# A two-block network on one core: the second block's tokens kept in residue-major order, and the low halves of the undilated keys kept twice

## The chip, the cores and the metric

The kernel runs on one core of a Trainium2 chip. The metric is the device time of one execution in microseconds (us). Three runs of the kernel before gave 2754.89, 2755.57 and 2758.86 us; their median, 2755.57 us, is the time that the change is measured against.

## The reference

A first block of two layers (a gated recurrent mixer, a convolution and a feed-forward part) turns 512 tokens of width 1024 into `x`. It is the same code before and after the change, up to its last norm. A second block follows, of two layers in float32. Their core is:

```python
def second_block(x, p, a_w_in, ...):
    cos, sin = rope_tables(x.shape[1])
    for i in range(2):
        h = mixer_a(x, ...) if i == 0 else mixer_b(x, ...)
        x = layer_norm(DEEPNORM_ALPHA * x + h, ln_g[i], ln_b[i])
        gate = sigmoid(x @ ple_w_gate[i])
        x = x + gate * (p[i] @ ple_w_proj[i])

def mixer_a(x, w_in, w_out, cos, sin):
    h = x @ w_in
    for gi, (window, dil) in enumerate(A_GROUPS):      # dil = 1, 4, 16
        q, k, v = ...                                  # 16 heads of 64, rope on q and k
        # tokens regrouped by their residue modulo dil, then a band of window // dil keys
        o, lse = banded_attention(strided(q), strided(k), strided(v), window // dil)
    o = the three groups' o, weighted by softmax(lse)
    return (o * silu(z)) @ w_out
```

`mixer_b` is a banded attention over neighbouring tokens (16 query heads, few key heads, a sink logit per head). So the undilated group of mixer A and mixer B look at blocks of 128 neighbouring tokens, while the groups with a stride look at tokens that are equal modulo 4.

## The kernel before

**Numbers.** Every float32 operand of a large product is split into a high and a low half of a narrower type (`split`: ScalarE copies the high half, VectorE subtracts it). A product of 128 rows of the contraction is three matmuls: high by high, high by low, low by high. A weight block comes by `wblock`: two loads of 512 KB into a ring of three `raw` tiles, each split into half of `hi` and `lo` when it has landed.

**Activations.** The input of mixer A is `HA = (Hh, Hl)`, feature-major: 8 tiles of 128 features by 512 tokens, high and low. The first block's last norm writes it in four chunks of 128 tokens (`chunkf`, `finish_T`): eight transposes of a chunk, and two splits into columns `128c` to `128c + 128`. The columns stand in the order of the tokens. `pend` holds these transposes back until a piece of mixer A asks for them (`pend.upto`).

**Mixer A** works through 12 steps, (Q, g): quads Q = 0 to 3 of four heads, and in each the groups g = 0 (undilated), 1 and 2 (dilated by 4 and 16; for both, keys are taken within a residue modulo 4, and a mask does the rest). A step (Q, g) has eight pieces of products, `a_pieces`: q and k, feature-major, two pieces each of 24 matmuls with 512 columns (weights stationary, tokens moving), and four pieces `v`, token-major, one for each block of 128 tokens, of 24 matmuls with 256 columns. In these the tokens are stationary:

```python
tk = slice(128 * b, 128 * b + 128) if g == 0 else slice(b, 512, 4)
tmj(lambda kc: (HA[0][:, kc, tk], HA[1][:, kc, tk]), wb[2], 0, 256, ps)
```

In g = 0 a block is 128 neighbouring columns, in g = 1 and 2 every fourth column. Step (0,0) does v first, then q and k; the others q and k first. Steps (1,0), (2,0), (3,0) do k before q.

Between a step's pieces `weave` puts the seven stages of the step before: scores with mask, maximum and exponentials of a head (`scores`: matmuls on PE, masked maximum on VectorE, exponentials on ScalarE), transposes of the exponentials, and the product with the values, whose result ScalarE evicts.

**Rotation.** When both halves of q or k are there, `rope` forms four products with cosine and sine on VectorE and two sums on POOL, and SP copies each in pieces of 32 partitions into the tile of heads. For g > 0 POOL's sum also reorders the tokens, from `4m+s` to `128s+m`. In the undilated steps of quads 1 to 3 `rope_split` does it with a split: q goes into two tiles `w`, where a head's high half stands beside its low half on 128 partitions; k goes into `kh`, with a head's high half kept twice, and `kl`, with its low half on 64 partitions. A score is then two matmuls: 128 rows (`kh`), and 64 rows (`kl`):

```python
return [(d[0][c][:, r, :], d[1][0][:, 2 * c + r, :]), (d[0][c][rows, r, :], d[1][1][rows, c, :])]
```

**What sets the order.** All DMAs, weights and these small copies alike, are issued by SP one after another (`ld`). A scheduler lays each engine's instructions in an order of its own when the program is built, so the order on ScalarE is not that of the code. The undilated results go to `o3`, those of g = 1 and 2 to tiles `w`; the results of a quad are weighted by `merge_stats` and the merges, which run beside the next quad. Where one group's layout differs from another's, the eviction or the merge reorders the tokens.

Then come the output product of mixer A, a layer norm, a gate, mixer B on the same scheme (undilated throughout, all its scores with 128 rows), and the same end, which writes the result.

Of the kernel before, what the change touches and what calls it, by code (L numbers as in the profile page):

```python
# [31 lines left out]
class Lane:  # L32
    """Background work: generators advanced a few steps at a time between foreground pieces."""
# [19 lines left out]
class Pending:  # L53
    """Deferred ends of a chain, run in order a few foreground pieces after their start."""
# [16 lines left out]
def emit(ctx, tc, a, out):  # L71
# [81 lines left out]
    # ---------------------------------------------------------------- helpers  # L153
# [42 lines left out]
    def fm_pair(wb, H, segs):  # L196
        """Both column chunks of a block, token range by token range as they become ready."""
# [17 lines left out]
    def wide(src, nk, lhs, chs, bank, use, pre=None, early=None, first=None):  # L215
        """Token-major product over 2*nk row blocks into 1024 columns, 512 columns and half of the rows at a time."""
# [24 lines left out]
    # ---------------------------------------------------------------- modulation  # L241
# [45 lines left out]
    def mod_start(pool, pool2, fill):  # L287
        """sh1 and sc1 of the first layer, streamed together."""
# [44 lines left out]
    def finish_T(pool, src, H, t0, A=None, B=None):  # L333
        """src: token-major chunk -> A*src+B, feature-major, split."""
        for i in range(2):
# [3 lines left out]
            if A is None:  # L339
                lasts["A"], lasts["V"] = split(H[0][:, 4 * i:4 * i + 4, t0:t0 + 128],  # L340
                                               H[1][:, 4 * i:4 * i + 4, t0:t0 + 128],
                                               pt.rearrange("p (m t) -> p m t", m=4))
                continue
# [15 lines left out]
    def rms(ss):  # L359
        """Reciprocal root mean square of each row."""  # L360
# [8 lines left out]
    def scaled(pool, xt, rs):  # L369
        """The rows times their factors, in two halves."""  # L370
# [46 lines left out]
    # ---------------------------------------------------------------- first block  # L417
# [3 lines left out]
    def projections(l, MIX, H, hook):  # L421
# [23 lines left out]
        # v and gates, chunk by chunk  # L445
# [18 lines left out]
        # convolution  # L464
# [29 lines left out]
        # gating unit  # L494
# [30 lines left out]
        def og_piece(h):  # L525
            """Output gate of one head."""
# [301 lines left out]
    def layer(l, H1, hside, oside, x_in, nn, mix_mods, ffn_mods):  # L828
# [83 lines left out]
        # output projection, second norm  # L912
# [46 lines left out]
        # feed forward  # L959
# [59 lines left out]
    # ---- start  # L1019
# [90 lines left out]
    def chunkf(h, c, xt, ss):  # L1110
# [6 lines left out]
        pend.add(c, lambda: finish_T(None, blocks(xt), h[1], 128 * c))  # L1117
# [4 lines left out]
    # ---------------------------------------------------------------- second block  # L1122
# [4 lines left out]
    def rope(RP, p1, p2, cs, perm, dst):  # L1127
        """p1, p2: [4 heads x 32, 512] halves; dst: [2 heads x 64, 2, 512]."""
# [14 lines left out]
    def rope_split(RP, p1, p2, cs, hi_to, lo_to):  # L1143
        """As rope, split; hi_to, lo_to: places (head, tile [128, slots, 512], first partition, slot) of the heads."""
# [14 lines left out]
    class Pair:  # L1159
        """Attention of two heads over 4 query blocks, in stages."""  # L1160
# [75 lines left out]
    def post_attention(i, Y, w_out, xin, sideh, first=None):  # L1236
# [8 lines left out]
        for c in range(4):  # L1245
            xt[c] = T(w6, [128, D], "w")
            ld(xt[c], xin[c])
# [556 lines left out]
```

## Time and profile before

| | |
|---|---|
| median of three runs | 2755.57 us (2754.89 to 2758.86) |
| span of the profiled execution | 2747.6 us |
| PE (TensorE matmuls) busy in it | 2669.2 us, 97% |
| VectorE, ScalarE, POOL busy | 1335.4, 965.2, 553.9 us (49%, 35%, 20%) |
| instructions in the span | 39361 |

The profile shows one execution. Its own time cannot be told from its span by what the trace holds; the median of the runs stands 8.0 us above the span, for what lies before the first and behind the last recorded instruction. PE is busy nearly all the time, so what the other engines do shows only where PE waits for it. `L138` is the one line that issues matmuls, `L121`, `L124` and `L159` are those that issue ScalarE's activations, tensor operations of VectorE and POOL, and DMAs, so groups are told apart by the names of their tiles: `mm` are accumulators of products (of `hi`, `lo` weights by `Hh`, `Hl`), `tr` those of scores and transposes, `md` those of the values, `sb` scores, `et` transposed exponentials.

### The profile page before, as it was taken

To read this page: it belongs to the slowest core of one execution; us is meant where nothing else is said; L and a number is where in the kernel's file an instruction comes from. 1 tells how busy PE (TensorE), PEld (TensorE's weight loads), DVE (VectorE), ACT (ScalarE), POOL (GpSimd) and SP (SyncE) were. 2 spreads that over 40 slices of the span, in tenths; PEclk is the share of its full clock that TensorE was granted. 3 is DMA by queue.
4 is the path that set the end of the run, shared out by engine and by line. 5 is a ranking of instruction groups with operands and counts; after the bars stand their busy time and mean duration, and the time that the engine had idled before them with its cause. 6 is when DMAs were issued, how large, how long until landed. Compare 5 with 4: busy or idle time off the path is not lost.

```text
span 2747.6 us, 39361 instructions
## 1 busy us (share of the span) xinstructions
PE 2669.2 (97%) x15288; PEld 2249.5 (82%) x15288; DVE 1335.4 (49%) x2802; ACT 965.2 (35%) x2017; POOL 553.9 (20%) x574
## 2 busy tenths in 40 slices
PE   7999999999999989999999999999999999999998
PEld 5888798778888878878788887887988888778786
DVE  5665744223332256565434334434535444675666
ACT  3323544111211153344322224324233333533753
POOL 1165531011011040043100002211302112021102
PEclk9999999999999999999999999999999999999999
DMA  8311644541222132145422223323323233425442
GB/s 295 116 62 53 203 147 156 194 140 62 63 67 70 51 109 69 62 141 197 146 92 92 93 92 130 97 77 108 108 77 108 83 110 100 142 95 155 121 166 77
DMA packets 125754, 311.04 MB, mean 113 GB/s; under 512 B 17120, under 2 KB 45376, under 8 KB 125568
## 3 DMA queue, kind: packets, MB, share of 16 engines
q1 hardware_dynamic: 125568, 308.53, 35.2%
q8 instruction: 121, 1.98, 0.3%
q14 instruction: 65, 0.53, 0.1%
HBM read 272.02 MB, written 13.89 MB: 104 GB/s over the span
## 4 chain that ended last, share of the span: by engine, by line
PE 82%; DVE 6%; DMA 4%; POOL 3%; ACT 3%; issue 2%; SPq 0%; POOLq 0%; DVEq 0%; ACTq 0%
PE mm L138 69%; PE tr L138 5%; PE md L138 5%; PE tr L1214 1%; DMA wm<-in_w_mod_dram 1%; DVE w L124 1%; DMA t<-mwd 1%; DVE lo L124 1%; POOL w L124 1%; ACT hi L121 1%; POOL rs L124 1%; ACT t L121 1%; POOL t L124 1%; DVE t L124 0%; DVE xs L131 0%
## 5 line engine op out<-in xcount | busy, mean ns | idle before, releaser
L138 PE MATMUL mm<-Hh,hi 128*128 128x512 f32 (+1 forms) x2168 | 790.9, 365 | 0.5 <-ACT Hh L121 0.4
L138 PE MATMUL mm<-Hl,hi 128*128 128x512 f32 (+1 forms) x2168 | 763.5, 363 | 0.0
L138 PE MATMUL mm<-Hh,lo 128*128 128x512 f32 (+1 forms) x2168 | 708.0, 364 | 0.0
L121 ACT ACTIVATE hi<-raw 128x1024 fp32r<-128x1024 f32 (+2 forms) x334 | 337.5, 1041 | 803.9 <-PE mm L138 445.3
L124 DVE TENSOR_TENSOR lo<-raw,hi 128x1024 fp32r<-128x1024 f32 (+2 forms) x334 | 429.1, 1305 | 317.7 <-ACT hi L121 317.5
L138 PEld LDWEIGHTS mm<-Hh,hi 128*128 128x128 f32 x2168 | 408.6, 189 | 96.9 <-issue 4.3
L138 PEld LDWEIGHTS mm<-Hl,hi 128*128 128x128 f32 x2168 | 408.4, 188 | 67.4 <-issue 0.6
L138 PEld LDWEIGHTS mm<-Hh,lo 128*128 128x128 f32 x2168 | 373.4, 189 | 47.4 <-issue 3.0
L124 POOL TENSOR_TENSOR w<-w,ot 128x256 f32<-128x256 f32 x160 | 128.5, 822 | 913.6 <-DVE ot L124 907.9
L124 DVE TENSOR_TENSOR sg<-mm,sg 128x512 f32<-128x512 f32 (+1 forms) x132 | 75.6, 599 | 408.9 <-PE mm L138 235.2
L138 PE MATMUL mm<-hi,Hh 128*128 128x256 f32 (+2 forms) x740 | 255.4, 346 | 6.5 <-ACT Hh L121 3.3
L138 PE MATMUL mm<-hi,Hl 128*128 128x256 f32 (+2 forms) x740 | 250.1, 338 | 1.0 <-POOL Hl L124 1.0
L138 PE MATMUL mm<-lo,Hh 128*128 128x256 f32 (+2 forms) x740 | 249.6, 337 | 0.0
L124 POOL TENSOR_TENSOR qr<-rt,rt 128x512 f32<-128x512 f32 x58 | 120.1, 2090 | 486.7 <-DVE rt L124 380.5
L138 PEld LDWEIGHTS mm<-hi,Hh 128*128 128x128 f32 x740 | 176.6, 239 | 15.6 <-ACT Hh L121 3.6
L138 PEld LDWEIGHTS mm<-hi,Hl 128*128 128x128 f32 x740 | 177.1, 239 | 6.3 <-issue 1.2
L138 PEld LDWEIGHTS mm<-lo,Hh 128*128 128x128 f32 x740 | 177.5, 240 | 3.3
L138 PE MATMUL mm<-hi,ah 128*128 128x512 f32 x352 | 140.0, 398 | 0.0
L138 PE MATMUL mm<-hi,al 128*128 128x512 f32 x352 | 139.7, 397 | 0.0
L138 PE MATMUL mm<-lo,ah 128*128 128x512 f32 x352 | 139.7, 397 | 0.0
L138 PE MATMUL mm<-hi,Yh 128*128 128x256 f32 (+1 forms) x416 | 128.6, 309 | 4.6 <-DVE t L124 2.7
L124 DVE TENSOR_TENSOR rt<-mm,cs 128x512 f32<-128x512 f32 x116 | 74.9, 684 | 116.7 <-PE mm L138 97.4
(364 smaller groups left out, 3708.8 us busy)
## 6 DMA issues: line engine op xcount, KB each, us to landing
raw<-in_w_gu_dram SPq DMA_DIRECT2D x88, 512.0 KB
raw<-in_a_in_dram SPq DMA_DIRECT2D x72, 512.0 KB
wm<-in_w_mod_dram SPq DMA_DIRECT2D x24, 1024.0 KB
raw<-in_w_in_dram SPq DMA_DIRECT2D x40, 512.0 KB
raw<-in_w_d_dram SPq DMA_DIRECT2D x40, 512.0 KB
raw<-in_w_mod_dram SPq DMA_DIRECT2D x36, 512.0 KB
t<-mwd SPq DMA_DIRECT2D x38, 256.0 KB
raw<-in_w_out_dram SPq DMA_DIRECT2D x16, 512.0 KB
```

Source lines behind the costliest of these rows:

```text
L121: return S.activation(o, i, f, **kw)
L124: return (e or V).tensor_tensor(out=o, in0=x, in1=y, op=op)
L138: lasts["P"] = PE.matmul(o, lhsT=l, rhs=r, start=start, stop=stop, **kw).ins
L1214: PE.transpose(pt[:, 128 * i:128 * i + 128], e, ident)
```

## The change

The second block keeps its 512 tokens in residue-major order: token 4m + s stands at column 128s + m. The norm's last transposes write `HA` so (`split_T`). The columns of one residue are then neighbours, and the V products of all groups take 128 neighbouring columns. In the undilated steps a V product now holds a residue, not a block: it goes to a tile `vr`, and 16 copies of 32 partitions, which SP issues, sort it into the blocks of `vb`. The rotation reorders in the undilated steps and in mixer B (from residues into blocks) and no longer in the dilated ones; evictions of undilated results reorder, those of the dilated ones don't. Inside a block of 128 tokens the order is now 4 times 32 (`in_blocks`), and mask and rotation tables are permuted to match on the host. Rows of tokens are read and written with a step of four where they pass through DRAM (`residue_rows`).

The low halves of the undilated keys (quads 1 to 3) are kept twice, in two tiles, so that both matmuls of a score have 128 rows. That takes 16 copies in the place of 8. The second matmul multiplies the whole q tile (high and low half) by the low half of the keys.

Step (0,0) no longer begins with V: a V chunk needs all four chunks of the norm. `first` does q and the first half of k, in two halves of 256 tokens (chunks 0 and 1 of the norm, then 2 and 3), reading `HA` and writing PSUM in runs of 32 columns, one for each block and residue; then come the second half of k, and V.

```diff
-        pend.add(c, lambda: finish_T(None, blocks(xt), h[1], 128 * c))
+        pend.add(c, lambda: split_T(blocks(xt), h[1], c))
...
+    def from_residue(z):
+        return z.rearrange("p (s b m) -> p b s m", s=4, b=4)
+    def in_blocks(z):
+        return z.rearrange("p (b s m) -> p b s m", s=4, b=4)
+    def residue_rows(t, c):
+        return t.rearrange("c (m s) d -> s (c m) d", s=4)[c]
+    def split_T(src, H, c):
+        for i in range(2):
+            pt = trt()
+            for m in range(4):
+                PE.transpose(pt[:, 128 * m:128 * m + 128], src(4 * i + m), ident)
+            hs = [h[:, 4 * i:4 * i + 4, :].rearrange("p k (s b m) -> p k b s m", s=4, b=4)[:, :, c] for h in H]
+            lasts["A"], lasts["V"] = split(*hs, pt.rearrange("p (k m s) -> p k s m", k=4, s=4))
...
-        pv = (lambda z: z.rearrange("p (m s) -> p s m", s=4)) if perm else (lambda z: z)
+        pv, po = (from_residue, in_blocks) if blocked else (lambda z: z, lambda z: z)
-            o = q.rearrange("p (s m) -> p s m", s=4) if perm else q
-            tt(o, pv(t[2 * i]), pv(t[2 * i + 1]), op, e=G)
+            tt(po(q), pv(t[2 * i]), pv(t[2 * i + 1]), op, e=G)
...
-            tt(q, t[2 * i], t[2 * i + 1], op, e=G)
+            tt(in_blocks(q), from_residue(t[2 * i]), from_residue(t[2 * i + 1]), op, e=G)
...
-                            t = T(AT, [128, 4, 512], "kh", F32R, bufs=1), T(AT, [128, 2, 512], "kl", F32R, bufs=1)
+                            kl = [T(AT, [128, 2, 512], n, F32R, bufs=2) for n in ("qs", "ks")]
+                            t = T(AT, [128, 4, 512], "kh", F32R, bufs=1), kl
-                                  [(hh, t[1], 64 * (hh % 2), hh // 2) for hh in range(4)]]
+                                  [(hh, kl[hh // 2], 64 * k, hh % 2) for hh in range(4) for k in range(2)]]
-                    rope(AT, d["p", i, 0], p2, cs, g > 0, t)
+                    rope(AT, d["p", i, 0], p2, cs, g == 0, t)
...
-                tk = slice(128 * b, 128 * b + 128) if g == 0 else slice(b, 512, 4)
-                pend.upto(b + 2)
-                tmj(lambda kc: (HA[0][:, kc, tk], HA[1][:, kc, tk]), wb[2], 0, 256, ps)
-                act(d["v"][:, b, :], ps, AF.Copy)
+                tmj(tok_lhs(HA, 128 * c), wb[2], 0, 256, ps)
+                act(d["vr"][:, c, :], ps, AF.Copy)
+                if g == 0:
+                    for b in range(4):
+                        ld(d["v"][32 * c:32 * c + 32, b, :], d["vr"][32 * b:32 * b + 32, c, :])
+        def first():
+            with behind("AV"):
+                wb[0] = wblock(a["a_in"][g, Q, 0], 8, 256)
+            wb[1] = wblock(a["a_in"][g, Q, 1], 8, 256)
+            ps = [mmt() for _ in range(3)]
+            for h in range(2):
+                for j, (i, m) in enumerate(((0, 0), (0, 1), (1, 0))):
+                    pend.upto(3 if h or j else 2)
+                    half = lambda z: from_residue(z)[:, 2 * h:2 * h + 2]
+                    hi, lo = (w[:, :, 128 * m:128 * m + 128] for w in wb[i])
+                    for kc in range(8):
+                        xh, xl = (half(z[:, kc, :]) for z in HA)
+                        mm(half(ps[j]), hi[:, kc, :], xh, kc == 0, False)
+                        mm(half(ps[j]), hi[:, kc, :], xl, False, False)
+                        mm(half(ps[j]), lo[:, kc, :], xh, False, kc == 7)
...
-        return vs + qks if (Q, g) == (0, 0) else qks + vs
+        if (Q, g) == (0, 0):
+            return [first, qk(1, 1)] + vs
...
-                        return [(d[0][c][:, r, :], d[1][0][:, 2 * c + r, :]), (d[0][c][rows, r, :], d[1][1][rows, c, :])]
+                        return [(d[0][c][:, r, :], d[1][0][:, 2 * c + r, :]), (d[0][c][:, r, :], d[1][1][c][:, r, :])]
...
-                    act(o3[2 * Q + c], pso, AF.Copy)
+                    act(from_residue(o3[2 * Q + c]), in_blocks(pso), AF.Copy)
-                    act(quad["o", g][:, c, :].rearrange("p (m s) -> p m s", s=4), pso.rearrange("p (s m) -> p m s", s=4), AF.Copy)
+                    act(quad["o", g][:, c, :], pso, AF.Copy)
...
-    act(vT, fm(zw["v"], 0, HB, SEGS_X)[0], AF.Copy)
+    act(in_blocks(vT), from_residue(fm(zw["v"], 0, HB, SEGS_X)[0]), AF.Copy)
...
-        ld(out[c][:, 256 * n:256 * n + 256], t[:, 256 * n:256 * n + 256])
+        ld(residue_rows(out, c)[:, 256 * n:256 * n + 256], t[:, 256 * n:256 * n + 256])
```

**SP's queue at the end of step (1,0).** In the kernel before, these copies stand between the second rotation of k (`kh`, `kl`), that of q (the tiles `w`) and the second half of the first weights of step (1,1) (the last row):

```order
L1157 DMA kh_15746<-qh_15775 32x512 x8
L1157 DMA kl_15747<-qr_15773 32x512 x4
L1157 DMA w_15882<-qh_15894 32x512 x2
L1157 DMA w_15883<-qh_15894 32x512 x2
L1157 DMA w_15882<-qr_15892 32x512 x2
L1157 DMA w_15883<-qr_15892 32x512 x2
L1157 DMA w_15882<-qh_15907 32x512 x2
L1157 DMA w_15883<-qh_15907 32x512 x2
L1157 DMA w_15882<-qr_15905 32x512 x2
L1157 DMA w_15883<-qr_15905 32x512 x2
L159 DMA raw_16120<-in_a_in_dram 128x1024
```

In the changed kernel the same place reads, without the `kh` row:

```order
L1171 DMA qs_15835<-qr_15867 32x512 x4
L1171 DMA ks_15836<-qr_15867 32x512 x4
L1171 DMA w_15980<-qh_15992 32x512 x2
L1171 DMA w_15981<-qh_15992 32x512 x2
L1171 DMA w_15980<-qr_15990 32x512 x2
L1171 DMA w_15981<-qr_15990 32x512 x2
L1171 DMA w_15980<-qh_16005 32x512 x2
L1171 DMA w_15981<-qh_16005 32x512 x2
L1171 DMA w_15980<-qr_16003 32x512 x2
L1171 DMA w_15981<-qr_16003 32x512 x2
L1376 DMA vb_16049<-vr_16050 32x256 x16
L159 DMA raw_16235<-in_a_in_dram 128x1024
```

Each rotation of k has four more copies (`qs` and `ks` hold the low keys), and the 16 copies that sort V into blocks stand ahead of the weights.

**ScalarE's order at the start of step (1,1).** Before, the second half of the step's first weights is split (`hi`, third row from the end) behind the first of four softmaxes (`sb`: the exponentials of one head are four activations):

```order
L121 ACTIVATE sb_16150,qst_15685<-sb_16150,qst_15685 128x128
L121 ACTIVATE sb_16150,qst_15685<-sb_16150,qst_15685 128x256
L121 ACTIVATE sb_16156,qst_15685<-sb_16156,qst_15685 128x256 x2
L121 ACTIVATE hi_16114<-raw_16120 128x1024
L121 ACTIVATE sb_16218,qst_15685<-sb_16218,qst_15685 128x128
L121 ACTIVATE sb_16218,qst_15685<-sb_16218,qst_15685 128x256
```

After, the same split (`hi`, the last row) stands behind the four softmaxes, two copies of transposed exponentials (`et`) and an eviction (`o`); the last seven rows up to it:

```order
L121 ACTIVATE sb_16368,qst_15774<-sb_16368,qst_15774 128x256
L121 ACTIVATE sb_16374,qst_15774<-sb_16374,qst_15774 128x256 x2
L121 ACTIVATE sb_16438,qst_15774<-sb_16438,qst_15774 128x128
L121 ACTIVATE sb_16438,qst_15774<-sb_16438,qst_15774 128x256
L121 ACTIVATE sb_16444,qst_15774<-sb_16444,qst_15774 128x256 x2
L121 ACTIVATE o_2_2021_14170<-md_16505 128x4x4x32
L121 ACTIVATE hi_16229<-raw_16235 128x1024
```

So the split that the second half of the first q products needs has moved from behind one softmax to behind all four.

**PE's order at the start of mixer A.** Before, the transposes of the norm's second chunk (`tr`, from a tile `w`) are followed by V products of 256 columns of the first chunk, 24 in all, among which the transposes of the third and fourth stand. The first rows:

```order
L338 MATMUL tr_14493<-ident,w_11413 128x128 x4
L338 MATMUL tr_14500<-ident,w_11413 128x128 x4
L138 MATMUL mm_14568<-hi_14557,Hh_14179 128x256
L138 MATMUL mm_14568<-lo_14558,Hh_14179 128x256
L138 MATMUL mm_14568<-hi_14557,Hl_14180 128x256
L138 MATMUL mm_14568<-hi_14557,Hh_14179 128x256
```

After, the third chunk's transposes follow at once, and q products in runs of 32 columns (`128x2x4x32`) stand among those of the fourth (from `w_11417`):

```order
L401 MATMUL tr_14493<-ident,w_11413 128x128 x4
L401 MATMUL tr_14500<-ident,w_11413 128x128 x4
L401 MATMUL tr_14580<-ident,w_11415 128x128 x4
L401 MATMUL tr_14587<-ident,w_11415 128x128 x4
L138 MATMUL mm_14577<-Hh_14179,hi_14557 128x2x4x32
L138 MATMUL mm_14577<-Hl_14180,hi_14557 128x2x4x32
L401 MATMUL tr_14618<-ident,w_11417 128x128 x4
L138 MATMUL mm_14578<-Hh_14179,hi_14557 128x2x4x32
L138 MATMUL mm_14578<-Hl_14180,hi_14557 128x2x4x32
L401 MATMUL tr_14625<-ident,w_11417 128x128 x2
```

Before, 24 products need only the first chunk; after, each product needs two chunks, and of the last chunk's eight transposes four stand behind two products, two behind four, and two (not shown) behind 26.

## Rows read from the trace of the kernel before

**Rows 1.** The page: span, busy time by engine, DMA rate of 40 slices, the chain.

```profile
span 2747.6 us, 39361 instructions
...
PE 2669.2 (97%) x15288; PEld 2249.5 (82%) x15288; DVE 1335.4 (49%) x2802; ACT 965.2 (35%) x2017; POOL 553.9 (20%) x574
...
GB/s 295 116 62 53 203 147 156 194 140 62 63 67 70 51 109 69 62 141 197 146 92 92 93 92 130 97 77 108 108 77 108 83 110 100 142 95 155 121 166 77
...
PE 82%; DVE 6%; DMA 4%; POOL 3%; ACT 3%; issue 2%; SPq 0%; POOLq 0%; DVEq 0%; ACTq 0%
```

**Rows 2.** Windows: length; busy us of PE, PEld, DVE, ACT, POOL; clock, DMA, GB/s.

```profile
1686.00:1690.10 4.10, 1.06 (x7) 0.68 (x7) 2.64 (x9) 2.12 (x6) 3.77 (x5) 1.00 0.31 109
1690.10:1693.50 3.40, 3.40 (x11) 2.77 (x10) 2.14 (x4) 2.12 (x6) 2.57 (x4) 0.50 0.38 154
...
1846.00:1889.00 43.00, 43.00 (x278) 36.60 (x274) 18.07 (x53) 18.41 (x51) 5.11 (x4) 1.00 0.32 84
1889.00:1953.00 64.00, 64.00 (x327) 53.84 (x324) 29.51 (x72) 20.47 (x51) 11.81 (x5) 0.97 0.39 119
```

**Rows 3.** The chain in order of time, 1815 to 1893: start, length, what.

```profile
1826.23 5.81 PE mm L138 x24
...
1833.65 5.62 PE mm L138 x24
...
1846.35 11.40 PE mm L138 x48
...
1873.02 3.02 PE mm L138 x24
...
1882.19 2.83 PE mm L138 x24
```

**Rows 4.** Weight loads by form: V of (0,2), then V of (1,0).

```profile
L138 PEld LDWEIGHTS mm<-lo,Hh 128*128 128x128 f32 x15 | 5.0, 330 | 0.0
...
L138 PEld LDWEIGHTS mm<-lo,Hh 128*128 128x128 f32 x15 | 2.8, 188 | 0.0
```

**Rows 5.** PE's timeline, 1893 to 1896: first, second and after eight.

```profile
1893.33 0.28 PE L138 MATMUL tr<-kh,w 128*128 128x256 f32 x1
1893.54 0.38 PE L138 MATMUL tr<-kl,w 64*128 64x256 f32 x1
...
1895.73 0.50 PE L138 MATMUL mm<-Hh,lo 128*128 128x512 f32 x1
```

**Rows 6.** The chain in order of time, mixer B: one pair's scores.

```profile
2537.58 1.92 PE tr L138 x16
```

**Rows 7.** SP's queue, 1846 to 1916: start, length, copies.

```profile
1860.61 4.95 SPq L1157 DMA_DIRECT2D kh<-qh  x8
...
1878.31 2.95 SPq L1157 DMA_DIRECT2D w<-qr  x4
1883.86 2.41 SPq L1157 DMA_DIRECT2D w<-qh  x4
...
1888.84 20.94 SPq L159 DMA_DIRECT2D raw<-in_a_in_dram  x6
```

**Rows 8.** Lines by form, 1889 to 1953: ScalarE's split and exponentials.

```profile
L121 ACT ACTIVATE hi<-raw 128x1024 fp32r<-128x1024 f32 x7 | 7.2, 1049 | 2.7 <-issue 2.1 <-ACT et L121 0.5
L121 ACT ACTIVATE sb<-sb,qst 128x256 f32<-128x256 f32 x12 | 5.9, 494 | 0.0
```

**Rows 9.** The chain in order of time, 1500 to 1800: step (0,0) begins.

```profile
1702.15 42.15 PE mm L138 x216
```

**Rows 10.** POOL's rotations by form, 1855 to 1890, then 1910 to 1930.

```profile
L124 POOL TENSOR_TENSOR qr<-rt,rt 128x512 f32<-128x512 f32 x4 | 5.1, 1289 | 49.9 <-DVE rt L124 46.2 <-DMA kl<-qr 3.7
...
L124 POOL TENSOR_TENSOR qr<-rt,rt 128x512 f32<-128x512 f32 x4 | 10.5, 2658 | 40.4 <-DMA raw<-in_a_in_dram 31.6 <-DVE rt L124 8.8
```

**Rows 11.** ScalarE's evictions by form, 1702 to 2372.

```profile
L121 ACT ACTIVATE w<-md 128x512 f32<-128x512 f32 x16 | 9.5, 592 | 4.5 <-PE md L138 4.5
L121 ACT ACTIVATE o<-md 128x512 f32<-128x512 f32 x8 | 4.7, 590 | 5.2 <-PE md L138 5.2
```

More of the change, by code (lines that the diff above doesn't have):

```diff
@@ L330, in behind, with finish_T @@
         return st
-    def finish_T(pool, src, H, t0, A=None, B=None):
+    def finish_T(pool, src, H, t0, A, B):
         for i in range(2):
@@ L1125, in emit, with rope @@
     x4 = scratch("x4", 4)
-    def rope(RP, p1, p2, cs, perm, dst):
+    def rope(RP, p1, p2, cs, blocked, dst):
         t = [T(RP, [128, 512], "rt", bufs=5) for _ in range(4)]
@@ L1246, in post_attention @@
             xt[c] = T(w6, [128, D], "w")
-            ld(xt[c], xin[c])
+            ld(xt[c], xin(c))
         def use(c, n2, ps):
@@ L1329, in f @@
                 if m == 0:
-                    with behind("AV" if (Q, g, i) == (0, 0, 0) else ""):
-                        wb[i] = wblock(a["a_in"][g, Q, i], 8, 256)
+                    wb[i] = wblock(a["a_in"][g, Q, i], 8, 256)
                     d["p", i, 0] = fm(wb[i], 0, HA, SEGS_X)[0]
@@ L1346, in f, with v @@
                     t = T(AT, [128, 2, 512], ("qs", "ks")[i], bufs=2)
-                    rope(AT, d["p", i, 0], p2, cs, g > 0, t)
+                    rope(AT, d["p", i, 0], p2, cs, g == 0, t)
                     d[i] = t
             return f
-        def v(b):
+        def v(c):
             def f():
-                if b == 0:
+                if c == 0:
                     wb[2] = wblock(a["a_in"][g, Q, 2], 8, 256)
                     d["v"] = T(A2, [128, 4, 256], "vb", bufs=2)
+                    d["vr"] = T(A2, [128, 4, 256], "vr", bufs=1) if g == 0 else d["v"]
@@ L1356, in f @@
                 ps = mmt()[:, 0:256]
-                tk = slice(128 * b, 128 * b + 128) if g == 0 else slice(b, 512, 4)
-                pend.upto(b + 2)
-                tmj(lambda kc: (HA[0][:, kc, tk], HA[1][:, kc, tk]), wb[2], 0, 256, ps)
-                act(d["v"][:, b, :], ps, AF.Copy)
-            return f
-        vs = [v(b) for b in range(4)]
-        qks = [qk(i, m) for i in ((1, 0) if g == 0 and Q else (0, 1)) for m in range(2)]
-        return vs + qks if (Q, g) == (0, 0) else qks + vs
+                tmj(tok_lhs(HA, 128 * c), wb[2], 0, 256, ps)
@@ new lines, in f @@
+                act(d["vr"][:, c, :], ps, AF.Copy)
+                if g == 0:
+                    for b in range(4):
+                        ld(d["v"][32 * c:32 * c + 32, b, :], d["vr"][32 * b:32 * b + 32, c, :])
+            return f
+        def first():
[13 more added lines that the diff above has]
+                        mm(half(ps[j]), lo[:, kc, :], xh, False, kc == 7)
+            d[0] = T(AT, [128, 2, 512], "qs", bufs=2)
+            rope(AT, ps[0], ps[1], cs, True, d[0])
+            d["p", 1, 0] = ps[2]
@@ L1367, in a_stages @@
+        vs = [v(c) for c in range(4)]
+        if (Q, g) == (0, 0):
+            return [first, qk(1, 1)] + vs
+        return [qk(i, m) for i in ((1, 0) if g == 0 else (0, 1)) for m in range(2)] + vs
     def a_stages(Q, g, d, quad):
@@ L1412, in merge_stats @@
         row = T(A2, [128, 512], "sb", bufs=4)[0:8, :]
-        act(row, pt[0:8, :], AF.Copy)
+        act(from_residue(row), in_blocks(pt[0:8, :]), AF.Copy)
         p2 = trt()
         for s_ in range(4):
-            PE.transpose(p2[:, 8 * s_:8 * s_ + 8], row[:, s_::4], ident[0:8, 0:8])
+            PE.transpose(p2[:, 8 * s_:8 * s_ + 8], row[:, 128 * s_:128 * s_ + 128], ident[0:8, 0:8])
         s0 = T(S2, [128, 2, 4, 4], "s0", bufs=1)
@@ L1624, in stats @@
             row = T(A2, [128, 512], "sb", bufs=4)[0:4, :]
-            V.tensor_copy(row, p3[0:4, :])
+            V.tensor_copy(from_residue(row), in_blocks(p3[0:4, :]))
             ld(rd[Q], row)
@@ L1708, in pack @@
     neg = lambda ok: np.where(ok, np.float32(0), -big).astype(np.float32)
+    tb = 4 * (s % 32) + s // 32
+    blk = lambda ok: neg(ok)[tb][:, tb]
     a["amask"] = np.concatenate([
-        neg(k >= q), neg(k <= q), neg(k >= q + 1), neg(k <= q), neg(k <= q), neg((k <= q) & (q % 4 == k % 4))], 1)
+        blk(k >= q), blk(k <= q), blk(k >= q + 1), blk(k <= q), neg(k <= q), neg((k <= q) & (q % 4 == k % 4))], 1)
     inv = (1.0 / (np.float32(10000.0) ** (np.arange(0, 64, 2, dtype=np.float32) / np.float32(64)))).astype(np.float32)
-    ang = (np.arange(512, dtype=np.float32)[:, None] * inv[None, :]).astype(np.float32)
+    tok = np.arange(512, dtype=np.float32).reshape(128, 4).T.reshape(-1)
+    ang = (tok[:, None] * inv[None, :]).astype(np.float32)
     a["cs"] = np.stack([np.tile(np.cos(ang).T, (4, 1)), np.tile(np.sin(ang).T, (4, 1))], 1).astype(np.float32)
```

15 lines of the change are left out of this document (5 added, 10 removed).

## The prediction

> **What bounds the kernel now.** The page comes first: TensorE (PE) is busy 97% of a span of 2747.6 us, and 82% of the chain that ended last is PE's [rows 1]. So an edit counts where it shortens PE's stream or makes PE wait; the other engines count where PE waits for them. The windows say where they have room: in 1889 to 1953, the fullest stretch of mixer A, VectorE is busy 29.5 of 64 us and ScalarE 20.5, and PE all of it [rows 2]. Mixer A, from about 1702 to 2370, is one unbroken run of PE work in the chain in order of time.
>
> Second view, that chain inside mixer A. The V products of a step are four pieces of 24 matmuls, 256 columns each. In step (0,2) they take 5.81, 5.81, 5.62 and 5.62 us, in step (1,0) 3.02, 3.01, 2.83 and 2.85 (one row of each length is shown) [rows 3]. Shapes and weights' sizes are the same; what differs is the stationary operand, every fourth token in (0,2), 128 neighbouring ones in (1,0). The weight loads show it by themselves: 330 ns with the step, 188 ns without [rows 4].
>
> Third, PE's timeline at the undilated scores of quads 1 to 3: products of 128 rows (kh) and of 64 rows (kl) take turns, 8 of them in 1895.73 - 1893.33 = 2.40 us, 0.30 us each [rows 5]. Mixer B has the same 256-column products with 128 rows throughout: 16 in 1.92 us, 0.12 each [rows 6].
>
> Fourth, the SP queue, since the change gives it more to issue: 8 copies of 32 rows take 4.95 us of it, a copy every 0.63 us, and one stretch of 40 copies ends only at 1888.84, when the next step's weights follow [rows 7].
>
> **What the change removes.** (a) *Strided V weights.* Groups 1 and 2 of four quads, 8 steps: a step's four pieces go from 2 x (5.81 + 5.62) = 22.9 to 2 x (3.02 + 2.83) = 11.7 us [rows 3]. 8 x 11.2 = **89.3 us**. PE is the bound there, so it all shows if the other engines follow: their work of a fast step is already done beside PE in 43 us in (1,0), VectorE 18 and ScalarE 18 us [rows 2]. The bounds are 0, if the step of the operand were not the cause, and 89.3.
>
> TensorE: Matmul & The Clock Gate, section LDWEIGHTS, of the Trainium skill counts a weight load by its columns alone; by that rule both loads would cost the same and the gain of (a) would be nothing. The two load rows differ by 142 ns at equal columns, so the trace decides against it here; it is kept as a rival.
>
> (b) *Alternating row heights.* With the low keys kept twice, both products have 128 rows. 3 quads x 4 calls x 8 products = 96, each 0.30 - 0.12 = 0.18 us less: **17.3 us** [rows 5, 6]. That a 128-row product costs 0.12 after another is a row of this program, so its lower bound is no less than about 15.
>
> Under Key Properties, TensorEngine Tiling of the Trainium skill says that a change of tiling mode drains the array; the rows agree, and (b) is that drain taken away.
>
> **What it adds.** (c) *SP's queue and the step after an undilated one.* A residue-major chunk of V must be sorted into token blocks: 16 copies per undilated step. The doubled low keys take 16 copies instead of 8 (quads 1 to 3). So between the k rotation of (1,0) and the second half of the next q weights stand 64 copies, not 40. Before, SP began them at 1860.61 and reached the weights at 1888.84, with a pause of 2.5 us for a rotation [rows 7]. After: 1888.84 + 24 x 0.63 - 2.5 = about 1901.5, and the 512 KB need 2 to 4 us more, estimated from the 295 GB/s of the page's first slice [rows 1] and a start-up.
>
> PE reaches that step at 1889.3 as before. The new PE order puts ahead of the second half 24 products (5.6 us at 0.234, as 11.40 us for 48 [rows 3]), four scores (4 x 0.96), their transposes (4 x 0.75) and the first values product (1.0): 13.5 us. ScalarE takes that weight half only behind the four softmaxes and the eviction (its order fence in the section on the change). A softmax is 3 x 0.49 + 0.40 and reads in between, 1.9 us, behind VectorE's 2 us; the first ends near 1899, the second 1901, two copies 1902, the others near 1904 and 1906, eviction 0.6, the half itself 1.05 [rows 8]: about 1908 for the first product that needs it. 1908 - 1889.3 - 13.5 = 5.2, with VectorE's share of the split about 5.5 us of idle PE, three times: **+16.5 us**. Bounds: 0, if the work fills the gap, and 24 x 0.63 = 15 us a time, 45 in all, if the whole backlog shows. In quad 0 the 16 copies come after the next q weights are loaded, and 11.4 us of q products [rows 3] cover their 10 us: 0.
>
> (d) *The first step.* V used to come first there, chunk by chunk: 24 products of chunk 0 were done while the last norm ran, and from 1702.15 PE needed 42.15 us for 216 products [rows 9]. Now q and half of k come first, in two halves of 256 tokens, and each half needs two chunks and the split of weights that ScalarE and VectorE take behind the last norm. Only 4 products stand ahead of most of the last chunk's transposes. From about 1702: 140 x 0.12 + 24 x 0.234 + 96 x 0.12 + 48 x 0.234 = 16.8 + 5.6 + 11.5 + 11.2 = 45.1 us; **+3 us**. PE was idle for most of 1686 to 1690.1 and its clock then fell to half until 1693.5 [rows 2]; with 2.9 us of products gone from 1694 to 1702 it may do so again: **+1 us**, 0 to 3.5.
>
> These 144 products read tokens and write PSUM in runs of 32 columns. No row of before has such a matmul. The nearest are contiguous ones at 0.12 us for 256 columns and the stepped loads that double: bounds 0 and 144 x 0.12 = 17 us. Runs of 128 bytes are nearer to contiguous than single elements with a step, so I take 0.
>
> SBUF — State Buffer of the Trainium skill, in the section on Door 1, gives SBUF lines of 16 bytes and PSUM lines of 8, and warns that any non-contiguous PSUM pattern slows matmuls much; by its warning (d) would be 17 us dearer. No run shows it yet.
>
> (e) *Rearranged copies.* POOL's rotations lose the step of four in groups 1 and 2 (2658 ns against 1289 in a contiguous step) and gain runs of 32 in undilated steps and mixer B; between 1.3 and 2.7 us each, hidden in mixer A by whole pieces of PE, and part of (c) where a step starts with one [rows 10]. Evictions only swap which of them is stepped: 590 and 592 ns, 0 [rows 11]. Row-stepped loads of xf and pp and the output move the same rows: 0. Contiguous merge transposes: 1 us at most, 0 taken.
>
> **The sum.** -89.3 - 17.3 + 16.5 + 3 + 1 = -86.1. The profiled span 2747.6 becomes 2661.5; the runs' median stands 8.0 above that span, for what lies around it, so 2755.6 becomes **2669.5 us**, own range 2658 to 2682.
>
> **Rivals.**
> *The gap of (c) fills or is short.* For it: the loads' arrival near 1905 is before ScalarE asks. Against: the new orders hold the second half behind four softmaxes. It gives 2669.5 - 16.5 = 2653. Chance 0.16.
> *Runs of 32 cost matmuls double, or (c) is up to 12 us a time.* +17 or +20: 2687 to 2690, both 2706. For it: stepped loads do double; against: runs are long, and PE's own work overlaps. Chance 0.21.
> *The step of the V operand is not the price.* Then (a) is 0 and the time 2759, no measurable change; (b) would only pay for (c) and (d). The load rule named above would give this. Against it are rows 3 and 4, which differ in nothing else. Chance 0.02.
> *SP's queue becomes the bound, slower than before.* Place: the copies between undilated keys and the next weights. If each of the 24 more took over 1.6 us, the three gaps would eat the 106.6 us won (3 x 24 x 1.6 = 115, less the 8 us of PE work that could still cover); at 2.5 us each they would be 180 us and the time about 2830. Against: 0.63 us in every stretch of such copies. Chance 0.02.
> The likeliest case has 0.59.
>
> **How the numbers follow.** The time is the likeliest case's, 2669.5. From 2648 (no gap, all of (a) and (b), nothing for (d)) to 2703 the range holds the first three cases but for the double mishap and some of their tails. No change that a measurement can tell is within 0.2%, 5.5 us. Faster 0.96 (the first three cases), same 0.02, slower 0.02.
>
> **What would show it.** (a): V pieces of groups 1 and 2 at 2.8 to 3.0 us, their loads at 188 ns. (b): eight score products in about 1 us. (c): PE idle of some 5 us after each of the three undilated steps, ended by ScalarE's split, SP's weights behind the V copies. (d): 256-column products at 0.12 us in the first step, or 0.24 if the second rival holds; a half clock after 1697. I am wrong if V pieces stay above 4 us, or if PE waits in steps (Q,1) and (Q,2) for weights or softmaxes that the longer V pieces covered.

## The result, and the profile after

The changed kernel takes **2671.67 us** (median of four runs, 2671.27 to 2673.18), the kernel before 2755.23 us (four runs, 2749.78 to 2758.86): a ratio of **0.9705, 95% interval 0.9691 to 0.9719**. The forecast was 2669.5 us. The profiled spans went from 2747.6 to 2669.2 us, 78.4 us less.

The page of the changed kernel, the lines that answer to [rows 1]:

```profile
span 2669.2 us, 39682 instructions
...
PE 2578.8 (97%) x15360; PEld 2166.1 (81%) x15360; DVE 1310.8 (49%) x2802; ACT 964.3 (36%) x2017; POOL 519.9 (19%) x574
...
PE 79%; DVE 7%; DMA 5%; ACT 3%; POOL 3%; issue 2%; SPq 1%; POOLq 0%; DVEq 0%; ACTq 0%
```

PE lost 90 us of busy time, but the span only 78: PE now waits in places where it did not, and SP's queue has come onto the chain of the last work.

**V.** Step (0,2) in the chain in order of time (start, length, what), and its weight loads by form; they answer to [rows 3, 4]:

```profile
1813.20 3.02 PE mm L138 x24
...
1822.36 2.83 PE mm L138 x24
```

```profile
L138 PEld LDWEIGHTS mm<-lo,Hh 128*128 128x128 f32 x32 | 6.0, 188 | 0.0
```

A V piece of a dilated step takes 3.0 and 2.8 us where it took 5.8 and 5.6, and a load 188 ns where it took 330.

**The undilated scores.** PE's timeline at the first of them, as [rows 5]:

```profile
1878.12 0.28 PE L138 MATMUL tr<-kh,w 128*128 128x256 f32 x1
1878.23 0.28 PE L138 MATMUL tr<-qs,w 128*128 128x256 f32 x1
1878.36 0.28 PE L138 MATMUL tr<-kh,w 128*128 128x256 f32 x1
```

From start to start a product takes 0.12 us, not 0.30.

**The wait behind it.** SP's queue there (as [rows 7]), and ScalarE's timeline at the same place; in brackets is the idle time ahead of an instruction and what ended it:

```profile
1877.94 10.05 SPq L1376 DMA_DIRECT2D vb<-vr  x16
1888.04 11.14 SPq L159 DMA_DIRECT2D raw<-in_a_in_dram  x6
```

```profile
1889.78 0.60 ACT L121 ACTIVATE o<-md 128x512 f32<-128x512 f32 x1 [0.37 <-PE md L138]
1892.25 1.06 ACT L121 ACTIVATE hi<-raw 128x1024 fp32r<-128x1024 f32 x1 [1.88 <-DMA raw<-in_a_in_dram]
```

The 16 sorting copies hold SP for 10 us; the second half of the next q weights is issued at 1888.04 and lands at 1892.23. ScalarE has been done with the softmaxes and the eviction for 1.88 us by then. Windows of this place, and of the first step (columns as [rows 2]):

```profile
1695.50:1702.50 7.00, 5.23 (x20) 3.84 (x20) 5.28 (x9) 5.36 (x10) 5.57 (x6) 0.51 0.37 150
...
1873.65:1893.30 19.65, 15.09 (x107) 11.93 (x107) 7.40 (x39) 10.98 (x38) 0.00 (x0) 1.00 0.39 107
1893.30:1896.70 3.40, 3.34 (x10) 2.00 (x11) 1.93 (x2) 2.28 (x5) 0.00 (x0) 0.53 0.61 212
```

PE is idle for 4.6 of 19.65 us, and the 3.4 us after it run at half clock (1.2 GHz), where [rows 2] has PE busy throughout. PE's waits from 1860 to 2300 (total us, times, longest); in the kernel before this view is empty there:

```profile
PE mm L138 <- ACT hi L121: 4.8, 3, 2.2
PE md L138 <- DMA vb<-vr: 3.8, 4, 1.4
PE tr L1228 <- ACT sb L121: 2.9, 6, 0.9
PE tr L1228 <- DVE mx L1201: 1.4, 3, 0.5
PE tr L1475 <- DVE mw L124: 0.5, 3, 0.2
```

**A quad's cycle.** In what follows it is the time on PE's timeline from the first product with `kh` of one quad to that of the next; after: 1878.12 to 2018.63, 140.5 us; before: 1893.33 to 2053.93, 160.6. It holds two dilated V steps and one quad's undilated scores. The change and its repeat, after_again, agree in it within 0.4 us.

### The profile page after: what moved, and what is told of

Read it like the earlier page. It is cut to its first block, busy times and chain, and to the rows that moved or that the text cites. A ratio compares the mean times of both kernels' runs of the same rounds, so it can differ in the third digit from the quotient of the medians.

```text
span 2669.2 us, 39682 instructions
## 1 busy us (share of the span) xinstructions
PE 2578.8 (97%) x15360; PEld 2166.1 (81%) x15360; DVE 1310.8 (49%) x2802; ACT 964.3 (36%) x2017; POOL 519.9 (19%) x574
## 4 chain that ended last, share of the span: by engine, by line
PE 79%; DVE 7%; DMA 5%; ACT 3%; POOL 3%; issue 2%; SPq 1%; POOLq 0%; DVEq 0%; ACTq 0%
PE mm L138 67%; PE md L138 5%; PE tr L138 5%; PE tr L1228 1%; DVE lo L124 1%; DVE w L124 1%; SPq L1376 1%; POOL w L124 1%; DMA wm<-in_w_mod_dram 1%; DMA t<-mwd 1%; ACT hi L121 1%; DMA raw<-in_a_in_dram 1%; POOL rs L124 1%; ACT t L121 1%; DVE xs L131 1%
## 5 line engine op out<-in xcount | busy, mean ns | idle before, releaser
L124 DVE TENSOR_TENSOR lo<-raw,hi 128x1024 fp32r<-128x1024 f32 (+2 forms) x334 | 422.3, 1286 | 299.2 <-ACT hi L121 298.8
L138 PEld LDWEIGHTS mm<-Hl,hi 128*128 128x128 f32 x2192 | 413.8, 189 | 66.7 <-issue 0.6
L138 PE MATMUL mm<-hi,Hh 128*128 128x256 f32 (+2 forms) x740 | 225.7, 306 | 6.5 <-ACT Hh L121 3.3
L138 PE MATMUL mm<-hi,Hl 128*128 128x256 f32 (+2 forms) x740 | 221.5, 300 | 0.5 <-POOL Hl L124 0.5
L138 PE MATMUL mm<-lo,Hh 128*128 128x256 f32 (+2 forms) x740 | 220.8, 299 | 0.0
L124 POOL TENSOR_TENSOR qr<-rt,rt 128x512 f32<-128x512 f32 x58 | 85.5, 1487 | 487.0 <-DVE rt L124 366.9
L138 PEld LDWEIGHTS mm<-hi,Hh 128*128 128x128 f32 x740 | 141.6, 192 | 15.3 <-ACT Hh L121 3.7
L138 PEld LDWEIGHTS mm<-hi,Hl 128*128 128x128 f32 x740 | 141.9, 192 | 6.1 <-issue 1.2
L138 PEld LDWEIGHTS mm<-lo,Hh 128*128 128x128 f32 x740 | 142.2, 192 | 3.7
```

Of the source, the lines that this page charges most:

```text
L124: return (e or V).tensor_tensor(out=o, in0=x, in1=y, op=op)
L138: lasts["P"] = PE.matmul(o, lhsT=l, rhs=r, start=start, stop=stop, **kw).ins
```

## The experiments

Cycles are from quad 1 to 2 and from 2 to 3. Each ratio is to the kernel before on the same chip; medians were taken on several chips, so compare ratios rather than medians. The values of before_vflat and nosort belong to other tokens, so these two price a part and are no replacement.

| kernel | median us | ratio (95%) | profiled span | cycles |
|---|---|---|---|---|
| before | 2755.23 | 1 | 2747.6 | 160.6, 160.7 |
| before_vflat | 2661.16 | 0.9686 (0.9670 to 0.9702) | 2657.5 | 138.3, 138.2 |
| before_kl_twice | 2743.61 | 0.9981 (0.9971 to 0.9992) | 2743.8 | 157.6, 159.1 |
| before_grouped | 2742.24 | 0.9975 (0.9965 to 0.9985) | 2740.6 | 156.5, 156.5 |
| the change | 2671.67 | 0.9705 (0.9691 to 0.9719) | 2669.2 | 140.5, 140.0 |
| after_again | 2669.77 | 0.9703 (0.9683 to 0.9723) | 2667.2 | 140.4, 139.6 |
| kl_once | 2668.20 | 0.9711 (0.9695 to 0.9728) | 2665.9 | 139.9, 140.0 |
| nosort | 2664.00 | 0.9692 (0.9677 to 0.9706) | 2661.8 | 137.0, 138.6 |
| sort_late | 2662.13 | 0.9672 (0.9654 to 0.9691) | 2659.9 | 138.1, 137.6 |
| hi_act | 2660.03 | 0.9664 (0.9644 to 0.9684) | 2660.2 | 136.4, 136.6 |
| grouped | 2665.98 | 0.9696 (0.9677 to 0.9715) | 2666.8 | 137.2, 137.2 |
| grouped_hi_act | 2667.81 | 0.9698 (0.9676 to 0.9720) | 2666.7 | 138.2, 135.9 |
| grouped_late | 2656.32 | 0.9665 (0.9650 to 0.9679) | 2661.3 | 135.5, 135.5 |

The cycle is the sharper measure: the part ahead of mixer A, which is the same code, takes some us more or less from one execution to the next, and whole runs of the kernel before spread over 9 us.

**V alone** (before_vflat).

```diff
-                tk = slice(128 * b, 128 * b + 128) if g == 0 else slice(b, 512, 4)
+                tk = slice(128 * b, 128 * b + 128)
```

> The kernel before with one edit: the V products of the dilated groups read 128 neighbouring tokens, as the undilated ones do (the values of those groups then belong to other tokens; nothing else is changed). If the step of the stationary operand is the whole price, 8 steps lose 11.2 us each and the time is 2755.2 - 89.3 = about 2666 us, with weight loads of V at 188 ns everywhere. If loads cost by their columns alone, nothing changes: 2755. If ScalarE or VectorE are then what PE waits for in the dilated steps, part of the 89 us comes back as idle time of PE: about 2690 to 2720.

Measured: 90.1 us less span (86 us by the ratio), and the cycle 22.3 us shorter, 11.2 for each of its V steps. The step of the stationary operand is the whole price, and nothing else comes to bound these steps. The changed kernel, with everything that the new order needs and the doubled keys, has a span 11.7 us longer than this one: all its other parts together cost time.

**The doubled low keys alone** (before_kl_twice): of the change, only the lines of `kl` and `kf`, put into the kernel before.

> The kernel before with the low keys of the undilated steps kept twice, and nothing else. The row-height theory: 96 score products at 0.12 instead of 0.30 us, 17.3 us less, so about 2738; SP has 8 copies more ahead of the next weights (5 us, three times), which PE's q products should cover, at most some 2 us a time coming back: 2738 to 2744. Rival: the copies' 5 us show in full three times, 15 us, and the doubling is worth nothing by itself: about 2753.

Measured: 5.2 us by the ratio, where 17.3 us of products went. The chain in order of time, at the place of [rows 7]:

```profile
1895.47 4.29 DMA raw<-in_a_in_dram
...
1899.78 1.06 ACT hi L121
...
1900.89 1.20 PE mm L138 x4
```

SP, eight copies later, issues the weights at 1895.47, and PE waits for them (4.6 us in three times in the view of waits, and 2.9 for softmaxes). The expected 2 us a time at most was too small: of 5.8 us the two cycles kept 3.0 and 1.5.

**The low keys once, in the changed kernel** (kl_once).

```diff
-                                  [(hh, kl[hh // 2], 64 * k, hh % 2) for hh in range(4) for k in range(2)]]
+                                  [(hh, t[1], 64 * (hh % 2), hh // 2) for hh in range(4)]]
...
-                        return [(d[0][c][:, r, :], d[1][0][:, 2 * c + r, :]), (d[0][c][:, r, :], d[1][1][c][:, r, :])]
+                        return [(d[0][c][:, r, :], d[1][0][:, 2 * c + r, :]), (d[0][c][rows, r, :], d[1][1][rows, c, :])]
```

> The changed kernel with the low keys kept once, as before: the second score product has 64 rows again, and SP has 8 copies less in each undilated step of quads 1 to 3. If SP's queue ahead of the next weights is what PE waits for there, 5.8 us more of PE's work and 5 us less of SP's fill the wait: the 17.3 us of slower products come back as 15 to 22 us less waiting, and the time is 2667 to 2674 us, that is, the doubling is worth next to nothing in this kernel. Rival: the wait is that of ScalarE's order behind the softmaxes, whatever SP does, and PE's products are paid in full: about 2689.

Measured: cycles of 139.9 and 140.0 us against 140.5 and 140.0, and PE's waits from 1860 to 2300 down from 13.6 us to 3.4, those for `hi` from 4.8 to 0.6:

```profile
PE tr L1474 <- DVE mw L124: 2.8, 3, 0.9
PE mm L138 <- ACT hi L121: 0.6, 3, 0.2
```

PE's slower products fill what was the wait. The doubling shortens PE's work by 5.8 us a quad and buys no time in this kernel.

**No sorting copies** (nosort), then **sorting copies behind the weights** (sort_late; `sorts` is a list that the next step's q piece empties when it has asked for its weights).

```diff
-                        ld(d["v"][32 * c:32 * c + 32, b, :], d["vr"][32 * b:32 * b + 32, c, :])
+                        sorts.append((d["v"][32 * c:32 * c + 32, b, :], d["vr"][32 * b:32 * b + 32, c, :]))
...
+                    while sorts:
+                        ld(*sorts.pop(0))
                     d["p", i, 0] = fm(wb[i], 0, HA, SEGS_X)[0]
```

> The changed kernel without the 16 copies that sort an undilated step's V into blocks (values then stand in residue order, so the undilated groups' results are of other tokens). SP reaches the next weights 10 us earlier, three times. If SP's queue is what PE waits for, the about 7.5 us of each undilated step's waiting shrink to 1 to 3: 2671.7 - 14 to 20 = 2652 to 2658 us. Rival: the waits come from scores that PE finishes sooner than the softmaxes follow, and stay: 2668 to 2672.

> The changed kernel with the sorting copies of V traced behind the weights of the next step's first q product; they then stand behind the second half of these weights on SP, 10 us later, and that half's split stands behind one softmax on ScalarE. If the sort costs only by standing ahead of the weights, this gives what leaving the copies out gave, a span of about 2662 us. If the values product then waits for the copies, they cost up to 3 us a time more: 2662 to 2670. If the load's place on SP doesn't matter, 2669.

Measured: 5 to 7 us less span without the copies than the change and its repeat, 7 to 9 with them behind the weights. Their place ahead of the weights is what they cost, as expected of sort_late, but that is a third of what the place loses (23 us, worked out below), not most of it as expected of nosort. What went are the values' wait for the sort (3.8 us) and one for VectorE's maximum (1.4 us); the wait for `hi` is still there in both, in nosort in this row from 1860 to 2300:

```profile
PE mm L138 <- ACT hi L121: 5.3, 3, 2.0
```

Waits of sort_late there:

```profile
PE mm L138 <- ACT hi L121: 5.5, 4, 1.5
PE tr L1228 <- ACT sb L121: 2.9, 6, 0.9
```

In both the weights still stand behind 48 copies where it was 40 before. In nosort SP issues them at 1878.17 and not at 1888.04, yet PE waits as long: the program's order there asks for them sooner, behind the scores of two heads and not of all four.

**The copies of high halves by ScalarE** (hi_act), with which SP issues the weights ahead of most copies.

```diff
-                    ld(dst[p0 + 32 * i:p0 + 32 * i + 32, sl, :].bitcast(F32), h[32 * hh:32 * hh + 32, :].bitcast(F32))
+                    by = S.dma_start if h is hi and aq else ld
+                    by(dst[p0 + 32 * i:p0 + 32 * i + 32, sl, :].bitcast(F32), h[32 * hh:32 * hh + 32, :].bitcast(F32))
```

> The changed kernel as it is, so that the others of this set stand beside it on the same chip: 0.970 of the kernel before, a span near 2669 us, the waits of PE at the starts of the dilated steps (Q,1) as in its profile.

> The changed kernel with the 24 copies of high halves of each undilated step of quads 1 to 3 (kh and w from qh) issued by ScalarE, which makes these halves, in the place of SP. SP then has 40 copies there, as in the kernel before, and the second half of the next weights stands ahead of the sorting copies. Theory: PE waits for that load and runs at half clock after the wait; with the load early both go, and of the 22.6 us that the three undilated steps lose against the sum without waits about 15 to 20 come back: a span of 2649 to 2654 us, no stretch at half clock in mixer A. ScalarE has 15 us more to do per step beside 43 us of PE. Rival: what holds PE up are the softmaxes behind scores that are now 5.8 us shorter, or ScalarE, which now issues copies too: 2665 to 2675.

Measured: 4.0 and 3.0 us a cycle less than after_again, little more than half of what was expected. The wait for `hi` is gone, and another has come, for transposed exponentials from ScalarE:

```profile
PE tr L138 <- ACT et L121: 3.7, 3, 1.2
PE tr L1229 <- ACT sb L121: 1.3, 2, 0.8
```

So both theories hold a part: the weights' place in SP's queue, and behind it ScalarE. No stretch of mixer A behind its first step is at half clock in this run, as expected.

**Fewer changes of row height instead of doubled keys** (before_grouped; grouped and grouped_hi_act are kl_once and the same order, the second with hi_act's edit).

```diff
+                turns = [(0, 0), (0, 2), (1, 0), (1, 2), (1, 1), (1, 3), (0, 1), (0, 3)]
...
+            for i, b in turns:
+                (q, k), (o, qs_, ks_) = qk[i], todo[b]
+                mm(o, q[:, qs_], k[:, ks_], b not in seen, len(qk) == 1 or b in seen)
+                seen.add(b)
```

> The kernel before with one edit: the eight score products of a head in the undilated steps of quads 1 to 3 stand in another order, so that products of 128 rows follow each other and products of 64 rows too (two to four changes of height a head in the place of eight); no copy is added. In the kernel before a pair of products took 0.62 us where two of one height take 0.24, so a change of height costs 0.19 us. Theory: a head's products take 1.3 to 1.7 us in the place of 2.5, 3 to 4.5 us less a quad, and since SP is no later, PE has its weights: 9 to 13 us in all, against the 4 us that keeping the low keys twice gave. Rival: PE waits behind shorter scores for ScalarE whatever SP does, and it gives 4 us or less, as the doubling did.

> The changed kernel with the low keys once (8 copies less on SP in each undilated step) and the score products in the order of two to four changes of height. With the low keys once and the old order the wait for the weights was just covered by PE's slower products (0.2 us of it left a time). Theory: what is now taken from the products, 3 to 4.5 us a quad, comes back in part as a wait for the same weights: a span of 2657 to 2666 us. Rival: products of one height in a row cost no less than alternating ones: 2666 and no wait.

> As the run before it, with the 24 copies of high halves issued by ScalarE, so that SP reaches the weights early. Theory: no wait for the weights, the sorting copies behind them, and the scores' gain in full: 3 to 4.5 us a quad below the kernel with the low keys once (span 2665.9), so about 2653 to 2657 us, less than any kernel so far. Rival: ScalarE, which has 15 us more to do, and its order set the pace: 2660, as with the doubled keys.

Measured: before_grouped loses 4.1 us of each cycle, all that the fewer changes give (a head's eight products take 1.33 us in the chain where they took 2.31, four heads a quad), and PE waits for nothing from 1860 to 2300:

```profile
1896.83 1.33 PE tr L138 x8
```

Doubled keys, which take more off the products (5.8 us), were worth 3.0 and 1.5. (Its whole time is 6.9 us less, not 12: in its profile mixer A's first scores begin 3.4 us later than in the profile of the kernel before, in code that is the same.) In grouped a wait for `hi` of 1.0 us a time is back, and the cycle is 2.8 shorter than kl_once's. With ScalarE as issuer (grouped_hi_act) it is no better: the cycles are 138.2 and 135.9 and the median 2667.81, worse than the rival's 2660. The wait for `hi` is gone and PE waits 2.2 us for transposed exponentials from ScalarE, which speaks for the rival's cause; that ScalarE sets the pace throughout is not shown.

**Grouped, with the sort behind the weights** (grouped_late).

> The changed kernel with the low keys once, the score products in the order of few changes of height, and the sorting copies of V traced behind the weights of the next step's first q product. SP has 32 copies ahead of these weights, less than the kernel before (40). From one kernel of two undilated steps' scores to the next, the kernel before took 160.6 us, with the V step taken away alone 138.3, with low keys once and grouped products 137.2, of which 1.0 was a wait for the weights. Theory: that wait goes and the clock with it, 135.5 to 136.2, three times, and the span is 2655 to 2663 us, as the first step's half clock lies at 10 or 7 us. Rival: the values product waits for the sort instead, 137 or more: 2664 to 2667.

Measured: 135.5 us in both cycles, and one short wait is left from 1860 to 2300:

```profile
PE tr L1486 <- ACT vb L121: 0.5, 3, 0.2
```

Four of its five runs took 2655.84 to 2656.34 us (the profiled one is the fifth, 2663.08), and the interval of its ratio lies below that of the change. It beats both kernels. Ahead of the weights SP has 40 copies, as in the kernel before (the 32 of the expectation is a miscount), where the change has 64.

**The price of a step** (steps): other tokens, one run.

```diff
+                tk = slice(128 * c, 128 * c + 128) if g == 0 else slice(256 * (c // 2) + c % 2, 256 * (c // 2) + 256, 2) if g == 1 else slice(c, 512, 4)
...
+                    flat = lambda z: z[:, 256 * h:256 * h + 256]
+                    step = lambda z: z[:, h::2]
+                    pairs = lambda z: z.rearrange("p (a h b) -> p a h b", h=2, b=2)[:, :, h]
+                    half, hout = ((step, flat), (flat, pairs), (flat, flat))[j]
```

> The changed kernel with other tokens read, for prices alone (the results are of other tokens): V of group 1 takes every second column as its stationary operand, V of group 2 every fourth, as before the change; of the three 256-column products of the first step, q's first half reads every second column of HA and writes PSUM in one piece, q's second half reads in one piece and writes PSUM in pairs of columns, and k's half does both in one piece. Theory: a stationary operand costs as many 16-byte lines as its columns touch, so a step of two costs no more than twice, and a step of four doubles: 0.24 us a product in group 2, and 0.12 to 0.24 in group 1. The rival, any step costs the same: 0.24 in both. For the moving operand and PSUM: 0.12 if they don't mind, up to 0.24 if each element is a line of its own.

Measured, weight loads by form in group 1 (every second column) and in group 2 (every fourth):

```profile
L138 PEld LDWEIGHTS mm<-lo,Hh 128*128 128x128 f32 x32 | 6.3, 197 | 0.0
...
L138 PEld LDWEIGHTS mm<-lo,Hh 128*128 128x128 f32 x32 | 10.6, 330 | 0.0
```

V pieces of group 1 took 3.0 to 3.1 us, those of group 2 5.7 to 5.8. And PE's timeline in the first step, at full clock, first with the moving operand at every second column, then with PSUM in pairs of columns:

```profile
1717.63 0.41 PE L138 MATMUL mm<-Hh,lo 128*128 128x256 f32 x1
1717.86 0.41 PE L138 MATMUL mm<-Hh,hi 128*128 128x256 f32 x1
1718.09 0.41 PE L138 MATMUL mm<-Hl,hi 128*128 128x256 f32 x1
...
1722.84 0.28 PE L138 MATMUL mm<-Hl,hi 128*128 128x256 f32 x1
1722.95 0.28 PE L138 MATMUL mm<-Hh,lo 128*128 128x256 f32 x1
1723.08 0.28 PE L138 MATMUL mm<-Hh,hi 128*128 128x256 f32 x1
```

0.23 us from start to start for the first, 0.12 for the second.

## Why the prediction was right, by its steps

**(a) V, 89.3 us: as worked out.** By the chain in order of time step (0,1) takes 36.68 us (1749.84 to 1786.52) where it took 47.93 (1744.30 to 1792.23), 11.25 less, and (0,2) 11.14 less; before_vflat, which does this alone, gives 90.1 of span. The rule of the Trainium skill that a load costs by its columns (TensorE: Matmul & The Clock Gate, section LDWEIGHTS) is refuted here for a step of four, 330 against 188 ns at 128 columns; for a step of two the difference is 9 ns.

**(b) Row heights, 17.3 us: right as PE's work, wrong as a gain.** 32 products a quad take 0.12 us each. But kl_once, without this, is as fast. The step that failed is that (b) and (c) were added as if apart: the products were the cover of the wait that (c) prices, and the eight copies more lengthen it.

**(c) The wait after an undilated step, 16.5 us: mis-sized, and its cause half wrong.** The cycle without waits would be 160.6 - 22.3 - 5.8 = 132.5 us; it is 140.5 and 140.0, so three such places cost about 23 us, if the third, behind the last cycle, costs what the two measured do. PE's waits there (the five kinds of over 0.3 us add up to 13.4 us) and half clock behind two of the three (3.4 us each, of which half is lost) make some 17 of them; the cause of the other 6 stays open. The prediction let ScalarE's order end the wait; the trace shows the weights landing 1.88 us after ScalarE was ready. SP was later than worked out: shifted by the 16.9 us that the step begins earlier, the issue was expected at 1884.6 and came at 1888.04, as SP still paused some 3 us for rotations. The clock after a wait, and the wait of the values for the sort (3.8 us), were not in the sum. That quad 0's sort would cost nothing holds: (0,1) lost all its 11.25 us.

**(d) The first step, 4 us: 5.5 measured.** Mixer A's first scores begin at 1749.77 (before: 1744.23). The chain there:

```profile
1705.34 6.20 DMA raw<-in_a_in_dram
...
1711.57 1.07 ACT hi L121
...
1712.68 37.17 PE mm L138 x240
```

From 1712.68 on 240 products took 37.17 us, as 0.12 and 0.234 us make them: runs of 32 columns cost nothing, and the rival that doubled them falls. The warning of the Trainium skill (SBUF — State Buffer, section on Door 1) that PSUM patterns that aren't contiguous slow matmuls much is not borne out by runs of 32 here, nor by pairs (steps). What came on top of the 4 us lies ahead of 1712.68 and is not seen singly: half clock lasted 6.8 us there, where it was 3.4 before, and PE waited 0.7 us for the split of a weight load.

**(e)** 0, measured 0.6: from the last transposes of mixer A's last merge on (line L1475, in the kernel before L1438), the kernel takes 377.9 us, before 377.3.

The sum of what was measured, -89.3 - 17.3 + 23 + 5.5 + 0.6 = -77.5, is the 78.4 of the spans, within 1 us; the forecast's was -86.1, 7.7 us too much. That the forecast came within 2.2 us of the median is luck, by a second error of the other sign: the 8.0 us between span and median are not what lies around the span, but came of a profiled execution that was faster than the three runs that the median was taken of. What lies around the span is 2.1 us in the changed kernel (a run of 2671.3 with the span 2669.2), which would make that execution 2749.7; the lowest of the four runs of before is 2749.78. With 2.1 in the place of 8.0 the forecast would have been 2663.6, and the result would have lain 8 us above it, still inside its own range.

## What to carry to other kernels

Where PE is the bound, look first at the layout of the stationary operand. It was worth more here than any order that was tried: a step of four floats doubled 768 small products, and writing the tokens in another order once took the step away, at a price of some 5 us where they are first used and of copies that sort them back. Before PE's work is shortened at a place, ask what arrives there: here small copies on the one DMA queue stood ahead of the next weights, and 5.8 us of saved products turned into a wait. In the kernel before, a saving that adds no copy (products of one height in a row, 4.1 us a cycle) was kept in full, where of a larger one by doubled data (5.8 us) about half or less was kept.

## What the runs showed of the hardware

A stationary operand at every second float cost next to nothing (197 against 188 ns a load), at every fourth 330 ns. A moving operand of 256 columns at every second float doubled its product, 0.23 us against 0.12. PSUM written in pairs of floats, or in runs of 32, took 0.12 us a product, as contiguous. A change between products of 128 and 64 rows cost 0.19 us, whichever way: in before_grouped the two starts at a change stand 0.21 and 0.22 us behind the start ahead of each, in a row of one height 0.12.

PE's clock was at half for 3.4 us behind the waits of step (1,1), and for 6.8 us in this profile's first step, 10.2 in that of after_again, with the same instructions. Half clock also came where the view shows no wait of PE, and then cost nothing: the kernel before has it three times from 1860 to 2300, 3.4 us each, amid strided V products, whose starts stand 0.23 to 0.24 us apart before it and in it. The first window of these (columns as [rows 2]):

```profile
1939.30:1942.70 3.40, 3.40 (x17) 3.09 (x17) 0.03 (x1) 0.38 (x1) 0.00 (x0) 0.50 0.00 0
```
